# A recurrence in a two-layer decoder step: earlier masked queries in the first chunk, and 17 filler steps moved to the last two chunks

## The chip, the cores and the metric

The kernel runs on one core of a Trainium2 chip. The metric is the device time of one execution in microseconds (us), and less is better. Five engines work side by side: TensorE (PE in the profile) multiplies matrices, VectorE (DVE) and ScalarE (ACT) do element-wise work, GpSimd (POOL) does some of it and issues DMAs, SyncE (SP) issues DMAs.

## What is computed

One inference step of a decoder with two layers. The first mixes the sequence with a matrix-state recurrence, the second with attention; a feed-forward part follows each. Only the first mixer matters here. The reference, cut to it:

```
p = xn @ w_in                       # q, k, v, output gate og, two small gates
C = w_c * C + sum_s w_g[s] * k[s] v[s]^T           # state, per chunk of the sequence
num = w_inter * (q @ C) + (q k^T * exp(decay)) @ v
h = num / max(|den|, exp(-m))
out = (rmsnorm(h) * sigmoid(og)) @ w_out
```

There are 8 heads with 64-wide keys and 128-wide values. The sequence is a lead-in of 16 rows and a prompt of 1024; beside it go 8 decode requests of 8 rows, each with a state of its own.

## The kernel before, in words

**The stage.** `recurrence` works through nine chunks. Chunk 0 has 80 rows (the 64 rows of the decode requests and the lead-in), chunks 1 to 8 have 128 rows each. For the rest of a chunk the steps are, in the order in which they are written:

- `chunk_scores`: q k^T into PSUM (`sps`, L1349), times the decays (`eb`, DVE, L1351); the keys transposed (`kps`, L1355) and weighted (`kw`, DVE, L1357); the queries scaled (`wb`, DVE, L1359). The scores of chunk i+1 are made before the output of chunk i.
- `chunk_state`: keys times values into PSUM (`cp`, L1388), added to the state `C` (DVE, L1392); the new state is multiplied by the chunk's decay on POOL (L1395) for the chunk after it.
- `chunk_out`: scores times values (`nps`, L1450) plus queries times state (L1454), two pairs of heads at a time; the denominators (`den`, DVE, L1412) and values (`vA`, ACT, L1420) are copied out, the exponentials of a later chunk follow (L1335), then the squares for the norm (L1469, `jk`).

Every third chunk `norm_heads` normalizes three chunks (L1528 to L1539, DVE).

**The first chunk** also serves the 8 decode requests, each with its own state. `first_queries` writes the scaled queries `wb` to a DRAM tile `qwD` (L1367, POOL), loads them back as `q2` in another layout with four DMAs (L1371, POOL) and clears two masked-query tiles (L1373, POOL; all of them are called `qq` in the profile). In `chunk_out` the DVE copies a head's part of `q2` into such a masked tile (L1433), and four matmuls per head multiply it with the requests' states (`nps<-C,qq`, L1438).

**The fills.** The products of the output gate, `p[og]`, are not made in a phase of their own. `gates_out` is a generator: 8 weight blocks (`whi`, `wlo`: a high and a low part, made from `wraw` at L256 to L260) by 3 column groups (336, 384 and 384 columns) by 8 contraction steps, 192 steps in all. A call `f(n)` in the recurrence puts n steps into PE's program at that place. A step is three matmuls (L193, L194, L195, into `mmA`). Behind the eighth step of a group, ACT takes the sigmoid from PSUM (`stg`, L955) and POOL writes it to DRAM (`ogD`, L956).

**The gates.** With the last chunks, `gate_head` (L1555) transposes one head's normalized values of three chunks into PSUM (`ghps`, three matmuls), DVE multiplies them by the stored sigmoid (L1556, into `ogqk` or `ogeb`, loaded at L971), and ACT and DVE split the result into two parts `xh`, `xl` (L271, L272), which the output projection reads. Ten gates stand in chunks 7 and 8. Gates and fills take their PSUM tiles from the same two banks: while a group of fills is unfinished it holds one of them, and all gates go through the other.

**What follows.** `mlp` loads the output weights (`wo` and `slot` from `woD`, L512, SP), eight pairs of 512 KB loads in a fixed order, and multiplies them (`pops`, L193 to L195). The tiles `wo` lie where the recurrence had its tiles: the first pair in the place of the last fill block's `wlo`, the third in the place of the `stg` tiles. So SP's first load waits for the last fill, and its third pair for the writes of the last sigmoids to `ogD`.

**The order.** PE, DVE, ACT and POOL run the recurrence in the order in which the code is written (`manual_schedule`); each engine works its own list in order and waits on semaphores. A place of an `f(n)` is thus a place in PE's list, and of its sigmoid and `ogD` write in ACT's and POOL's.

Of the kernel before, what the change touches and what calls it, by code (L numbers as in the profile page):

```python
# [12 lines left out]
ALU = mybir.AluOpType  # L13
# [4 lines left out]
P = 128  # L18
D = 1024
KT = D // P  # L20
# [8 lines left out]
NT = len(TT)  # L29
# [849 lines left out]
@_add(Net)  # L879
def phase_a(self, vt):  # L880
    nc, I, O = self.nc, self.I, self.O
    w_in = I["w_in_a"][0]
    qkD = self.dram.tile([8, P, T], F32, name="qkD")
    ogD = self.dram.tile([8, P, T], F32, name="ogD")
# [266 lines left out]
@_add(Net)  # L1151
def recurrence(self, kp, rec, v, qkD, fill, gate):


    nc, I, O = self.nc, self.I, self.O
    eD, wD, cap, cap0, wcP, wcS, bm = rec
    tm, den, ssq = self.fin

    self.fills = 0

    def f(n):
        for _ in range(n):
            next(fill, None)
            self.fills += 1

    C = self.C
    E = mybir.EngineType
    with ExitStack() as cr, self.pool("recAp", bufs=2, space=PSUM) as pp:
        order = ExitStack()
        order.enter_context(self.tc.manual_schedule(engines={E.PE, E.DVE, E.Activation, E.Pool}))  # L1170
        args = (pp, kp, C, v, qkD, eD, wD, tm)

        r0 = cr.enter_context(self.pool("rec0"))
        sets = {1: r0}
        load = lambda i: self.chunk_load(i, sets[i % 3], *args)
        with self.pool("sampA") as sp:
            R = self.chunk_load(0, r0, *args)
            N = dict(eb=r0.tile([P, HA, P], F32, name="eb1", tag="eb", bufs=2))
            self.first_load(R, sp)
            f(4)  # L1180
            self.chunk_decay(0, R, tm, cap0)
            R["exp"]()
            f(6)
            self.chunk_scores(0, R, r0, *args, f)
            self.first_queries(R, sp)
            f(2)
            self.first_sums(R, pp)
            self.first_keys(0, R, bm)
            f(3)
            self.chunk_state(0, R, *args, wcP, f)  # L1190
            N = self.chunk_load(1, r0, *args, **N)
            self.chunk_out(0, R, r0, *args, den, ssq, f, sp)

            ahead = r0.tile([P, HA, P], F32, name="eb2", tag="eb", bufs=2)
            nc.gpsimd.dma_start(ahead, eD[:, TT[2][0] : TT[2][1]].partition_broadcast(P))
            self.first_states(R, sp, pp, v, wcS, bm, f, self.decay_steps(1, N, tm, cap), N)
        with self.pool("rec2") as sets[2], self.pool("rec1", bufs=2) as rp, self.pool("rec3") as sets[0]:
            R, N = N, self.chunk_load(2, sets[2], *args, eb=ahead, loaded=True)
            self.chunk_decay(2, N, tm, cap)
            N["exp"]()  # L1200
            f(10)
            self.chunk_scores(1, R, rp, *args, f)
            g, norm = f, iter(())
            places = []
            gate = gate(places)
            for i in range(1, NT):
                N2 = load(i + 2) if i + 2 < NT else None
                if i + 1 < NT:
                    f(12 if i == 1 else 3)
                    self.chunk_scores(i + 1, N, rp, *args, f)  # L1210
                next(norm, None)
                g(2)
                self.chunk_state(i, R, *args, wcP, g)
                if i == NT - 1:
                    state = self.last_state(C[i % 2], pp, rp)
                    next(state)
                if N2:
                    self.chunk_decay(i + 2, N2, tm, cap)
                next(norm, None)
                self.chunk_out(i, R, rp, *args, den, ssq, g, exp=N2 and N2["exp"],  # L1220
                               then=(lambda: next(state, None)) if i == NT - 1 else None)
                for _ in norm:
                    pass
                norm = self.norm_heads(i // 3, v, rp) if i % 3 == 2 else iter(())
                if i in (6, 7):

                    for x in ("qk", "eb"):
                        y = sets[i % 3].tile([P, 1024], F32, name=f"og{x}{i}", tag=x,
                                             bufs=2 if x == "eb" and i == 7 else None)
                        places += [y[:, z : z + GL] for z in (0, 512)]  # L1230
                    gate(-1)
                if i == 6:
                    while self.fills < 3 * KT * KT - KT:
                        f(1)

                    def g(n):
                        if i == NT - 1:
                            f(2)
                        gate(0) or gate(1)
                R, N = N, N2  # L1240
            f(1000)
            order.close()
            for _ in norm:
                pass
# [93 lines left out]
@_add(Net)  # L1338
def chunk_scores(self, i, R, rp, pp, kp, C, v, qkD, eD, wD, tm, f):

    nc = self.nc
    L = TT[i][1] - TT[i][0]
    qk, eb, qw = R["qk"], R["eb"], R["qw"]

    sps = [pp.tile([P, 4, P], F32, name=f"sps{i}{g}", tag="sps") for g in range(2)]
    for j in range(4):
        for g in range(2):
            r = slice(g * 64, g * 64 + 64)
            nc.tensor.matmul(sps[g][:L, j, :L], qk[r, 4 + j, :L], qk[r, j, :L], start=True, stop=True)  # L1349
    for g in range(2):  # L1350
        nc.vector.tensor_tensor(out=eb[:L, g::2, :L], in0=sps[g][:L, :, :L], in1=eb[:L, g::2, :L], op=ALU.mult)  # L1351
    f(2 if i else 6)
    kps = pp.tile([P, 4, P], F32, name=f"kps{i}", tag="sps")
    for j in range(4):
        nc.tensor.transpose(kps[:L, j, :], qk[:, 4 + j, :L], self.ident)  # L1355
    kw = R["kw"]
    nc.vector.tensor_tensor(out=kw[:L], in0=kps[:L].rearrange("p j (a k) -> p (j a) k", a=2),  # L1357
                            in1=tm[:L, i, 64:72].unsqueeze(2).broadcast_to([L, HA, DK]), op=ALU.mult)
    nc.vector.tensor_tensor(out=qw[:, :, :L], in0=qk[:, :4, :L], in1=qw[:, :, :L], op=ALU.mult)  # L1359


@_add(Net)
def first_queries(self, R, sp):

    nc = self.nc
    qd = self.dram.tile([P, 4, NS], F32, name="qwD")
    nc.gpsimd.dma_start(qd, R["qw"][:, :, :NS])  # L1367
    q2 = R["q2"]
    for a in range(2):
        for z in range(2):  # L1370
            nc.gpsimd.dma_start(q2[a * 64 : a * 64 + 64, :, z, :], qd[z * 64 : z * 64 + 64])  # L1371
    for qm in R["qms"]:
        nc.gpsimd.memset(qm, 0.0)  # L1373


@_add(Net)
def chunk_state(self, i, R, pp, kp, C, v, qkD, eD, wD, tm, wcP, f):

    nc = self.nc
    Cn, Cw = C[i % 2], C[2]  # L1380
    s = slice(NS, T0) if i == 0 else slice(0, P)
    for z in range(2):
        js = slice(2 * z, 2 * z + 2)
        ps = pp.tile([P, 2, DV + 1], F32, name=f"cp{i}{z}", tag="cps")
        for x in range(2):
            for a in range(2):
                h = 2 * (2 * z + x) + a
                nc.tensor.matmul(ps[a * 64 : a * 64 + 64, x, :], R["kw"][s, h, :], v(i)[s, h, :], start=True, stop=True)  # L1388
        if i == 0:
            nc.scalar.copy(Cn[:, js, :], ps)  # L1390
        else:
            nc.vector.tensor_tensor(out=Cn[:, js, :], in0=Cw[:, js, :], in1=ps, op=ALU.add)  # L1392
    if i + 1 < NT:

        nc.gpsimd.tensor_tensor(out=Cw, in0=Cn, in1=wcP[:, :, i].unsqueeze(2).broadcast_to([P, 4, DV + 1]),  # L1395
                                op=ALU.mult)


@_add(Net)
def chunk_out(self, i, R, rp, pp, kp, C, v, qkD, eD, wD, tm, den, ssq, f, sp=None, exp=None, then=None):  # L1400
# [8 lines left out]
    def done(ps, g, hs):  # L1409

        hx = slice(hs[0], hs[0] + 3, 2)
        nc.vector.tensor_copy(den[:L, i, hx], ps[:L, :, DV])  # L1412
        if i == 0:
            y = R["y"][g]
            nc.scalar.copy(y[:L], ps[:L, :, :DV])
            nps.append((y, hx))
            for x, h in enumerate(hs):
                nc.scalar.activation(R["jk"][:L], y[:L, x], AF.Square, accum_out=ssq[:L, 0, h : h + 1])
        else:
            nc.scalar.copy(v(i)[:L, hx, :DV], ps[:L, :, :DV])  # L1420

    new = lambda g: pp.tile([P, 2, DV + 1], F32, name=f"nps{i}{g}", tag="nps")
    if i == 0:
        for g, hs in enumerate(((0, 2), (4, 6), (1, 3), (5, 7))):
            f(4)
            ps = new(g)
            for x, h in enumerate(hs):
                o = ps[:L, x, :]
# [8 lines left out]
                for j in range(4):  # L1437
                    nc.tensor.matmul(o, qm[:, j * T0 : (j + 1) * T0], R["C0"][:, j, h, :], start=False, stop=(j == 3))  # L1438
            done(ps, g, hs)
    else:  # L1440

        for z in range(2):
            f(2 if z == 0 else 3)
            if z:
                f(3)
            ps = [new(2 * z + a) for a in range(2)]
# [1593 lines left out]
```

## Time and profile before

| | us |
|---|---|
| time, median of 3 runs | 2832.24 (2831.84 to 2833.01) |
| profiled execution, its own time | 2829.72 |
| its span | 2828.0 |
| PE busy in the span | 2761.9 (98%) |
| the recurrence with its fills and gates, `sps` of chunk 0 to the first `pops` | 244.3 to 428.3 of the span |
| PE idle between 235 and 455 by the waits it names | 7.9 |

Times in a row are us from the start of the span. A row of the timeline shows start, duration, engine, line, operation, output, inputs and shape; a bracket at its end is the idle time of the engine ahead of it and what ended it. Neighbours of one kind are shown as one row with their count. `PEclk` is the granted TensorE clock, 1.00 being full speed.

### The profile page before, as it was taken

The page shows a single profiled execution, that of the slowest core. Times are in us where ns is not written, and L with a number is a line of the kernel's source. Part 1 is how long each engine was busy: PE and PEld are TensorE (multiplying, and loading weights), DVE is VectorE, ACT ScalarE, POOL GpSimd, SP SyncE. Part 2 cuts the span into 40 slices and gives each one's busy share as a digit, 9 for nine tenths or more (in the row PEclk, how much of TensorE's full clock was granted, in tenths as well). Part 3 has the DMA queues.
Part 4 walks back from the last instruction along what each step waited for, and adds up shares of the span by engine and source line. Part 5 has one row for each costly group of instructions (what it writes and reads, how often), then busy time and mean ns, then how long its engine had stood idle before and what let it go on. Part 6 is the DMA issues. An engine that isn't in the chain of part 4 may idle for free. (4 is left out here: it accounts for less than half of the span.)

```text
span 2828.0 us, 60538 instructions
## 1 busy us (share of the span) xinstructions
PE 2761.9 (98%) x23543; PEld 2650.3 (94%) x23543; DVE 1800.4 (64%) x4025; ACT 1177.3 (42%) x2299; POOL 836.0 (30%) x1313
## 2 busy tenths in 40 slices
PE   8999999999999999999999999999999999999998
PEld 8989889999999999999999888677999999999998
DVE  4632566888887765563455444777388888766556
ACT  5422453432322334443444445777343223323345
POOL 3122233132232332124453202544313223323111
PEclk9999999999999999999999999999999999999999
DMA  6666547245554375545444676442524555527556
GB/s 196 171 196 162 144 125 255 90 143 165 176 167 148 112 243 174 195 145 171 139 172 132 237 279 226 154 143 86 157 83 128 175 176 164 161 90 239 178 191 215
DMA packets 439001, 474.03 MB, mean 168 GB/s; under 512 B 41422, under 2 KB 365258, under 8 KB 437690
## 3 DMA queue, kind: packets, MB, share of 16 engines
q1 hardware_dynamic: 387522, 320.78, 36.8%
q0 software_dynamic: 43808, 143.17, 15.3%
q10 hardware_dynamic: 7384, 6.22, 0.7%
q8 instruction: 185, 3.03, 0.5%
q14 instruction: 102, 0.84, 0.1%
HBM read 322.84 MB, written 147.21 MB: 166 GB/s over the span
## 5 line engine op out<-in xcount | busy, mean ns | idle before, releaser
L1611 PE MATMUL m<-xh,slot 128*128 128x276 f32 x2752 | 541.3, 290 | 1.8 <-ACT fs L1640 1.8
L1611 PEld LDWEIGHTS m<-xh,slot 128*128 128x128 f32 x2752 | 440.4, 188 | 3.6 <-ACT fs L1640 2.2
L1611 PE MATMUL m<-xl,slot 128*128 128x276 f32 x1376 | 397.4, 289 | 0.0
L1611 PEld LDWEIGHTS m<-xl,slot 128*128 128x128 f32 x1376 | 259.1, 188 | 0.0
L193 PE MATMUL tmps<-slot,xh 128*128 128x256 f32 (+2 forms) x864 | 243.1, 281 | 0.0
L195 PE MATMUL tmps<-slot,xl 128*128 128x256 f32 (+2 forms) x864 | 240.6, 278 | 0.0
L194 PE MATMUL tmps<-slot,xh 128*128 128x256 f32 (+2 forms) x864 | 240.5, 278 | 0.0
L272 DVE TENSOR_TENSOR slot<-slot,slot 128x1024 fp32r<-128x1024 f32 x124 | 162.9, 1314 | 60.7 <-ACT slot L271 59.2
L271 ACT CAST slot<-slot 128x1024 fp32r<-128x1024 f32 x124 | 129.6, 1046 | 141.2 <-PE m L1611 111.7
L194 PEld LDWEIGHTS tmps<-slot,xh 128*128 128x128 f32 (+1 forms) x864 | 159.2, 184 | 0.1
L195 PEld LDWEIGHTS tmps<-slot,xl 128*128 128x128 f32 (+1 forms) x864 | 158.6, 184 | 0.0
L193 PEld LDWEIGHTS tmps<-slot,xh 128*128 128x128 f32 (+1 forms) x864 | 158.4, 183 | 0.2
L193 PE MATMUL mmA<-xh,whi 128*128 128x384 f32 (+1 forms) x384 | 135.1, 352 | 0.0
L194 PE MATMUL mmA<-xl,whi 128*128 128x384 f32 (+1 forms) x384 | 127.9, 333 | 0.0
L195 PE MATMUL mmA<-xh,wlo 128*128 128x384 f32 (+1 forms) x384 | 127.7, 333 | 0.0
L272 DVE TENSOR_TENSOR slot<-vA,slot 128x1024 fp32r<-128x1024 f32 (+1 forms) x59 | 82.2, 1396 | 32.6 <-ACT slot L271 31.5
L272 DVE TENSOR_TENSOR slot<-Ht,slot 128x1024 fp32r<-128x1024 f32 (+1 forms) x59 | 81.4, 1382 | 32.3 <-ACT slot L271 31.1
L271 ACT CAST slot<-Ht 128x1024 fp32r<-128x1024 f32 (+1 forms) x59 | 61.0, 1037 | 96.8 <-PE m L1611 92.9
L271 ACT CAST slot<-vA 128x1024 fp32r<-128x1024 f32 (+1 forms) x59 | 60.8, 1035 | 95.5 <-PE m L1611 90.5
L1715 DVE TENSOR_TENSOR ws<-ws 128x128 f32<-128x128 f32 x264 | 93.8, 355 | 8.9
L2862 ACT ACTIVATE s<-s,nb 128x272 f32<-128x272 f32 (+7 forms) x126 | 98.9, 786 | 0.0
L2897 ACT COPY th<-tp 128x768 f32<-128x768 f32 (+1 forms) x80 | 73.6, 920 | 53.7 <-PE tp L2889 30.5
(805 smaller groups left out, 8668.8 us busy)
## 6 DMA issues: line engine op xcount, KB each, us to landing
ws<-in_w_down SPq DMA_DIRECT2D x176, 128.0 KB, 2.8
sD<-ws SPq DMA_DIRECT2D x176, 128.0 KB, 2.3
slot<-sD SPq DMA_DIRECT2D x40, 512.0 KB, 4.2
slot<-in_w_gate_up SPq DMA_DIRECT2D x36, 512.0 KB, 3.9
kp<-in_cache_k SPq DMA_DIRECT2D x32, 512.0 KB, 6.7
vp<-in_cache_v SPq DMA_DIRECT2D x32, 512.0 KB, 5.1
vA<-in_w_gate_up SPq DMA_DIRECT2D x26, 512.0 KB, 4.4
Ht<-in_w_gate_up SPq DMA_DIRECT2D x26, 512.0 KB, 3.9
```

Source lines behind the costliest of these rows:

```text
L193: mm(ps, sh, mh, start=first, stop=False)
L194: mm(ps, sh, ml, start=False, stop=False)
L195: mm(ps, sl, mh, start=False, stop=last)
L271: self.nc.scalar.copy(hi, src)
L272: self.nc.vector.tensor_tensor(out=lo, in0=src, in1=hi.bitcast(F32), op=ALU.subtract)
L1611: nc.tensor.matmul(u.ps[h, b], w[p][:, k], x[q][:, k], start=first and k == i == 0, stop=k == 3 and i == 2, skip_group_check=True)
L1715: tt(out=o, in0=a, in1=b, op=ALU.subtract)
L2862: nc.scalar.activation(ss[z, u], ss[z, u], AF.Exp, bias=nb[:, z : z + 1], accum_out=sm[:, u, z : z + 1])
L2897: nc.scalar.copy(th.rearrange("p x z (u h q) -> p h (x z u) q", h=2, q=64)[:, :, :n], pt[:, :, :n])
```

## The change

Six edits, all in the recurrence:

1. The call ahead of the next chunk's scores goes from 12 to 10 steps (chunk 1) and from 3 to 2 (the others); the one ahead of a chunk's first outputs from 2 to 1 (chunks 1 to 6); in chunk 0 each of four groups from 4 to 3.
2. The loop that ran all fills but the last eight at once in chunk 6 is gone, and a gate in chunks 7 and 8 has `f(2)` ahead of it (before: in chunk 8 only).
3. In chunk 0 the scaling of the queries (`wb`) stands ahead of the keys' transposes and weighting instead of behind them.
4. In `first_queries` the two clears stand between the write of `qwD` and its four loads, and the loads are in the order in which the heads need them.
5. In chunk 0 POOL's scaling of the state is issued behind the second group of outputs instead of ahead of the first.
6. An unused name in `phase_a`.

```
-                    f(12 if i == 1 else 3)
+                    f(10 if i == 1 else 2)
...
                 if i == 6:
-                    while self.fills < 3 * KT * KT - KT:
-                        f(1)
 
                     def g(n):
-                        if i == NT - 1:
-                            f(2)
+                        f(2)
                         gate(0) or gate(1)
...
+    scale = lambda: nc.vector.tensor_tensor(out=qw[:, :, :L], in0=qk[:, :4, :L], in1=qw[:, :, :L], op=ALU.mult)
+    if i == 0:
+        scale()
     f(2 if i else 6)
...
-    nc.vector.tensor_tensor(out=qw[:, :, :L], in0=qk[:, :4, :L], in1=qw[:, :, :L], op=ALU.mult)
+    if i:
+        scale()
...
-    for a in range(2):
-        for z in range(2):
-            nc.gpsimd.dma_start(q2[a * 64 : a * 64 + 64, :, z, :], qd[z * 64 : z * 64 + 64])
     for qm in R["qms"]:
         nc.gpsimd.memset(qm, 0.0)
+    for z in range(2):
+        for a in range(2):
+            nc.gpsimd.dma_start(q2[a * 64 : a * 64 + 64, :, z, :], qd[z * 64 : z * 64 + 64])
...
-        nc.gpsimd.tensor_tensor(out=Cw, in0=Cn, in1=wcP[:, :, i].unsqueeze(2).broadcast_to([P, 4, DV + 1]),
-                                op=ALU.mult)
+        decay = lambda: nc.gpsimd.tensor_tensor(out=Cw, in0=Cn, in1=wcP[:, :, i].unsqueeze(2).broadcast_to(
+            [P, 4, DV + 1]), op=ALU.mult)
+        if i:
+            decay()
+        else:
+            R["decay"] = decay
...
-            f(4)
+            f(3)
...
+            if g == 1:
+                R["decay"]()
...
-            f(2 if z == 0 else 3)
+            f(1 if z == 0 else 3)
```

POOL in chunk 0, from the write of `qwD` on; first before, then with the change:

```order
L1367 DMA qwD<-wb_3080 512x1x64
L1371 DMA qq<-qwD 64x4x64 x4
L1373 MEMSET qq 128x400 x2
L1395 TENSOR_TENSOR C_107<-C_105,wcP 128x516
L1279 DMA qk_3246<-qkD 128x8x128
```

```order
L1369 DMA qwD<-wb_3080 512x1x64
L1372 MEMSET qq 128x400 x2
L1375 DMA qq<-qwD 64x4x64 x4
L1277 DMA qk_3245<-qkD 128x8x128
L1276 DMA eb_3086<-eD 128x8x128
L1281 DMA wb_3246<-wD 64x4x128 x2
L957 DMA ogD<-stg_3261 128x384
L1396 TENSOR_TENSOR C_107<-C_105,wcP 128x516
```

The clears moved ahead of the loads, and the scaling of the state behind them, three prefetches and an `ogD` write.

PE from the fifth gate to the sixth, between chunk 7's outputs and chunk 8's state; before, where the three `mmA` matmuls are the last fill step of all:

```order
L1555 MATMUL ghps_4818<-ident,vA 128x80
L1555 MATMUL ghps_4818<-ident,vA 128x128 x2
L193 MATMUL mmA_4666<-xh,whi_4353 128x384
L194 MATMUL mmA_4666<-xl,whi_4353 128x384
L195 MATMUL mmA_4666<-xh,wlo_4354 128x384
L1555 MATMUL ghps_4852<-ident,vA 128x80
L1555 MATMUL ghps_4852<-ident,vA 128x128 x2
```

With the change, where the first three finish a group (`mmA_4716`) and the next three begin the last one (`mmA_4824`):

```order
L1562 MATMUL ghps_4790<-ident,vA 128x80
L1562 MATMUL ghps_4790<-ident,vA 128x128 x2
L193 MATMUL mmA_4716<-xh,whi_4446 128x384
L194 MATMUL mmA_4716<-xl,whi_4446 128x384
L195 MATMUL mmA_4716<-xh,wlo_4447 128x384
L193 MATMUL mmA_4824<-xh,whi_4446 128x384
L194 MATMUL mmA_4824<-xl,whi_4446 128x384
L195 MATMUL mmA_4824<-xh,wlo_4447 128x384
L1562 MATMUL ghps_4828<-ident,vA 128x80
L1562 MATMUL ghps_4828<-ident,vA 128x128 x2
```

Two steps stand there now, and the group that they finish has its sigmoid (`stg_4821`) on ACT at this place, behind chunk 7's last cast and squares:

```order
L271 CAST xh<-ogqk_4647 128x336
L1476 ACTIVATE jk_4797,ssqA<-vA 128x128
L1476 ACTIVATE jk_4801,ssqA<-vA 128x128
L1476 ACTIVATE jk_4805,ssqA<-vA 128x128
L1476 ACTIVATE jk_4809,ssqA<-vA 128x128
L956 ACTIVATE stg_4821<-mmA_4716 128x384
L271 CAST xh<-ogqk_4647 128x336
L271 CAST xh<-ogeb_4648 128x336
```

PE at the end of the recurrence, from the last outputs of chunk 8 to the output projection (`pops`); before:

```order
L1454 MATMUL nps_4910<-C_106,wb_4546 128x129
L1454 MATMUL nps_4911<-C_106,wb_4546 128x129
L1555 MATMUL ghps_4924<-ident,vA 128x128 x3
L1258 MATMUL nnpP<-ident,nnP 4x128
L193 MATMUL pops_5037<-xh,wo_293_5007 128x276
L194 MATMUL pops_5037<-xl,wo_293_5007 128x276
L195 MATMUL pops_5037<-xh,wo_293_5007 128x276
```

With the change:

```order
L1461 MATMUL nps_4904<-C_106,wb_4492 128x129
L1461 MATMUL nps_4905<-C_106,wb_4492 128x129
L193 MATMUL mmA_4824<-xh,whi_4446 128x384
L194 MATMUL mmA_4824<-xl,whi_4446 128x384
L195 MATMUL mmA_4824<-xh,wlo_4447 128x384
L1562 MATMUL ghps_4924<-ident,vA 128x128 x3
L1256 MATMUL nnpP<-ident,nnP 4x128
L193 MATMUL pops_5037<-xh,wo_293_5007 128x276
```

The last fill step of all stands here now, one gate ahead of the projection. Of the 192 steps, 191 stood ahead of the first gate before; 175 do now (173 of them ahead of chunk 8's `kps`).

More of the change, by code (lines that the diff above doesn't have):

```diff
@@ L881, in phase_a @@
     nc, I, O = self.nc, self.I, self.O
+    E = mybir.EngineType
     w_in = I["w_in_a"][0]
```

## The prediction, made before the changed kernel ran

> **What bounds the kernel now.** I read the page first.
>
> ```profile
> span 2828.0 us, 60538 instructions
> PE 2761.9 (98%) x23543; PEld 2650.3 (94%) x23543; DVE 1800.4 (64%) x4025; ACT 1177.3 (42%) x2299; POOL 836.0 (30%) x1313
> ```
>
> PE is busy for 98% of the span, and the change removes no matmul and adds none. It can only change PE's idle time and the time PE runs at a lower clock. All six edits lie between the first chunk and the output projection, so I read PE's waits there, from 235 to 455 us (columns: waiting line and what it waited for; us in total, times, longest).
>
> ```profile
> PE nps L1438 <- POOL C L1395: 2.3, 1, 2.3
> PE ghps L1555 <- DVE ogeb L1556: 2.1, 2, 1.2
> PE ghps L1555 <- DVE ogqk L1556: 2.0, 3, 1.1
> PE nps L1450 <- ACT vA L1420: 1.5, 3, 1.0
> ```
>
> That is 7.9 us in four groups: the first chunk's masked queries (2.3), the ten gates (4.1) and the copies of outputs (1.5, of which 1.0 in chunk 8). So the tail of gates holds 5.1 us, the first chunk 2.3, the chunks between 0.5. The clock comes next, by stretches of 3.41 us (first number: the length, then PE's busy time; PEclk is the granted clock).
>
> ```profile
> 254.27:257.68 3.41, 1.56 (x11) 1.27 (x9) 0.99 (x1) 0.49 (x1) 3.41 (x6) 1.00 0.28 79
> 257.68:261.09 3.41, 2.93 (x13) 2.96 (x14) 1.12 (x4) 0.00 (x0) 3.41 (x6) 0.50 0.48 131
> 418.11:421.52 3.41, 2.26 (x27) 1.90 (x23) 1.75 (x10) 2.95 (x8) 0.49 (x2) 1.00 0.89 258
> 421.52:424.93 3.41, 1.51 (x12) 0.91 (x11) 2.61 (x9) 1.21 (x4) 2.31 (x4) 1.00 1.03 419
> 424.93:428.34 3.41, 3.41 (x21) 2.88 (x19) 1.82 (x5) 1.29 (x4) 0.00 (x0) 0.50 1.02 389
> ```
>
> Where PE was busy for 1.56 and 1.51 us of a stretch, the next one ran at half clock; where it was busy for 2.26, the next did not. A half-clock stretch with PE busy throughout costs half of 3.41, **1.7 us**; the one behind the first stall costs half of its busy 2.93, 1.5. The bill of before in this stage is 2.3 + 1.5 + 0.5 + 5.1 + 1.7 = **11.1 us**. I now write the same bill for the changed kernel.
>
> **The first chunk (edits 3, 4, 5, and f(4) to f(3)).**
>
> ```profile
> 247.29 0.88 DVE L1351 TENSOR_TENSOR eb<-sps,eb 80x320 f32<-80x320 f32 x2
> 249.55 0.48 DVE L1359 TENSOR_TENSOR wb<-qk,wb 128x320 f32<-128x320 f32 x1
> 249.33 0.54 POOL L956 DMA_DIRECT2D ogD<-stg  x1 [3.31 <-ACT stg L955]
> 250.84 0.74 POOL L1367 DMA_DIRECT2D qwD<-wb  x1 [0.97 <-DVE wb L1359]
> 253.51 2.48 POOL L1371 DMA_DIRECT2D qq<-qwD  x4 [1.92 <-DMA qwD<-wb]
> 255.97 0.82 POOL L1373 MEMSET qq<- 128x400 f32 x2
> 256.75 1.06 POOL L1395 TENSOR_TENSOR C<-C,wcP 128x516 f32<-128x516 f32 x1
> 256.69 2.21 DVE L1433 COPY qq<-qq 64x32 f32<-64x32 f32 x4 [5.56 <-DMA qq<-qwD]
> 253.47 0.34 PE L193 MATMUL mmA<-xh,whi 128*128 128x384 f32 x1
> 254.00 0.34 PE L193 MATMUL mmA<-xh,whi 128*128 128x384 f32 x1
> 258.16 1.98 PE L1438 MATMUL nps<-C,qq 128*80 128x129 f32 x8 [2.33 <-POOL C L1395]
> 261.16 1.04 PE L1438 MATMUL nps<-C,qq 128*80 128x129 f32 x8
> ```
>
> (The two `mmA` rows are the starts of two fill steps in a row: a step of 384 columns takes 0.52 us, and so one of 336 some 0.46.) The first masked product starts at 258.16, after 2.33 us of waiting, and takes 1.98 where the next takes 1.04: the half clock. The row names POOL's state scaling, but the chain behind it is longer: scaled queries (DVE), write to DRAM, landing, four loads, landing, copies into the masked tile. With edit 3 the scaled queries are there at about 248.6 (behind 247.29 + 0.88, and 0.48 of their own, instead of behind `kps` and `kw` at 249.55), and POOL then waits for nothing between its `ogD` write (249.33 + 0.54) and `qwD`: the whole 0.97 of its row goes. The landing of `qwD` and the loads move by as much. The clears (0.82) fall into the 1.92 us in which POOL waits for that landing, so they cost nothing there; were the landing earlier, they would cost 0.82. The loads go out one each 0.62 us (2.48 for 4), and the order lets the first head go on two of them: 256.69 less 0.97 gives the first data at 255.7, the two copies end near 256.2, and the scaling of the state no longer stands on POOL ahead of them. PE, with one fill step (0.46) less in this group, arrives at 258.16 - 2.33 - 0.46 = 255.4. The wait is **0.8 to 1.0**, I take 0.9, and too short for a half clock by the rows above. The gain is 2.3 + 1.5 - 0.9 = 2.9 us. The moved scaling of the state costs nothing: nothing in chunk 0 reads it, and the other half of chunk 0's outputs and the requests' states lie between it and chunk 1; without that cover it would cost its 1.06.
>
> **The middle chunks (one step less ahead of the scores, one less ahead of the outputs).** Two steps of 0.52 us, 1.04 per chunk, leave PE's list, while the element-wise chain stays.
>
> ```profile
> 372.58 0.72 PE L1454 MATMUL nps<-C,wb 64*128 64x129 f32 x8
> 376.77 1.29 DVE L1351 TENSOR_TENSOR eb<-sps,eb 128x512 f32<-128x512 f32 x2 [3.22 <-ACT eb L1335]
> 377.77 0.60 PE L1355 MATMUL kps<-ident,qk 128*128 128x128 f32 x4
> 377.98 1.22 DVE L260 TENSOR_TENSOR wlo<-wraw,whi 128x1024 fp32r<-128x1024 f32 x1
> 401.11 1.16 PE L1450 MATMUL nps<-vA,eb 128*128 128x129 f32 x8 [0.27 <-ACT vA L1420]
> ```
>
> From the end of a chunk's outputs (372.58 + 0.72 = 373.30) the exponentials take until 376.77, and `kps` overwrites a bank that L1351's first half (0.65) has to read: it can go at 377.4, 4.1 us behind the outputs. PE reached it at 4.47, and with a step less reaches it at 3.95. That is 0.15 to 0.25 us a chunk; for six chunks **1.2 us** (0 if the exponentials come sooner as well, 2 if also the state's matmuls wait). In the chunks with a norm (3 and 6) the outputs already waited for the copies (0.27 at 401.11, and as much in chunk 3: the two make 0.5 of the 1.5 us in the list of waits), so no cover is left: chunk 3 waits its 0.25 and most of the two steps, **1.1**; in chunk 6 the split of the last weight block (L260, 1.22 us on DVE), which stood earlier, now falls in as well, **1.8** (1.3 without it).
>
> **Chunks 7 and 8 (edit 2).** Here 18 steps, 9.4 us of PE work, come behind `kps` of chunk 8, two ahead of nearly every gate.
>
> ```profile
> 407.84 0.46 PE L1555 MATMUL ghps<-ident,vA 80*128 80x80 f32 x3
> 408.22 1.10 PE L1388 MATMUL cp<-vA,kw 128*64 128x129 f32 x16
> 415.73 0.51 PE L1555 MATMUL ghps<-ident,vA 80*128 80x80 f32 x3
> 428.31 0.38 PE L193 MATMUL pops<-xh,wo 128*128 128x276 f32 x1
> 409.84 0.47 ACT L271 CAST xh<-ogqk 128x336 fp32r<-128x336 f32 x1 [1.33 <-DVE ogqk L1556]
> 418.81 0.19 ACT L1469 ACTIVATION_READ_ACCUMULATOR jk<-vA 128x1 f32 x1
> 419.01 1.28 ACT L955 ACT_TABLE_LOAD   x1
> 420.30 0.49 ACT L955 ACTIVATE stg<-mmA 128x384 f32<-128x384 f32 x1
> ```
>
> The old waits of up to 1.2 us for a previous gate's DVE step are covered by two steps (1.04) but for some 0.15 at each of four gates, **0.6** in all (0 to 1). But two gates now need the bank of a group that has just ended, so they wait for a sigmoid. The second gate: ACT casts the first gate's head at 409.84, then loads its table (1.28) and runs the sigmoid (0.49), until 412.1; PE arrives 3.5 us behind 407.84 (two steps 1.04, gate 0.4, state 1.1, one step of each width 0.98) at 411.3: **1.0** with the hand-over. The sixth gate: its sigmoid stands behind chunk 7's squares, which end at 419.0, 3.3 us behind the fifth gate's start (415.73), and takes 0.49: 3.8. PE is there after the gate and two steps, some 1.7 us: **2.1**. A stretch around that wait may have PE busy for less than 1.6; I give a half clock there 0.7, so **1.1**.
>
> **The weights of the projection.**
>
> ```profile
> SPq L512 <- PE mmA L195: 37.5, 1, 37.5
> SPq L512 <- DMA ogD<-stg: 7.2, 1, 7.2
> DMA to landing us min/median/max: 9.4/9.4/9.4
> slot<-in_w_gate_up SPq DMA_DIRECT2D x36, 512.0 KB, 3.9
> ```
>
> SP's load of the first `wo` pair waited 37.5 us for PE's last fill step, and then had from 416.8 to 428.3 before PE needed it: 11.5 us, in which PE did the sixth to the tenth gate and chunk 8. Now the last step stands one gate (0.5 us) ahead of `pops`, so PE waits for the load. A 512 KB load takes 3.9 us elsewhere, and a second at 419 GB/s (the stretch at 421.52) 1.25 more: 5.2. The upper end is the 9.4 us of these very loads among others. The row of 3.9 has the same queue and size, and SP has nothing ahead of this pair, so I stay near the lower end: 5.3, less the gate 0.5, **4.8** (4.6 to 8.9). Such a gap halves the clock: **1.7**. The third pair waits for the last sigmoid's write to `ogD` (7.2 us of waiting in before), which now comes later too: **0.7** (0 to 3).
>
> **The sum.** After: 0.9 + 1.2 + 1.1 + 1.8 + 0.6 + 1.0 + 2.1 + 1.1 + 4.8 + 1.7 + 0.7 = 17.0 us, against 11.1: **+5.9 us**. From the profiled execution, 2829.7 (span 2828.0 and 1.7 around it), that is 2835.6; it lies 2.5 below the median of the runs, 2832.2, so for the median I forecast **2838.1**.
>
> The Trainium skill, "TensorE: Matmul & The Clock Gate", Part 1, has the clock halved after an idle window of about 3.4 us. The trace disagrees: a wait of 2.33 us sufficed. By the rule only the wait for the weights goes cold, the sum is 1.1 lower, 2837.0, just on the near side of the bound below.
>
> **The rivals.**
> - *The tail is filled, and the weights come in time* (not slower). If the first `wo` load doesn't hang on the last fill step, the 4.8 + 1.7 + 0.7 go, and if ACT runs the sigmoids early, 2.1 + 1.1 as well: 17.0 - 10.4 = 6.6, so -4.5, 2828; with the sigmoids waited for, -1.3, 2831. It decides at a landing within 0.5 us of the last step. For it: the idle gaps of the tail are real, 5.1 us. Against it: the 37.5 us row.
> - *The middle chunks keep their cover.* Where the exponentials move up with PE, the 1.2 + 1.1 + 1.8 stay at 0.5: +2.3, 2834.5. For it: `kps` had 0.4 us to spare. Against it: 0.4 is less than a step, and at 401.11 there was nothing to spare.
> - *The weights are late and stay late.* The load shares the queues (DMA share 1.03 at 421.52) and takes 9.4: 8.9 - 4.8 = 4.1 more, and with the third pair at 2 it is +11.3, 2843.5.
> - *The queries don't come sooner.* If the landings set the start and not the issue, the first chunk keeps 2.3 + 1.5: +2.9 on the forecast, 2841. The two landings in a row speak for it; the removed 0.97 against.
>
> **How the numbers follow.** The forecast 0.48 (2835 to 2841, half of it above the bound), the tail filled 0.14, the middle covered 0.14, the weights late 0.16, the queries late 0.08. The bound that a measurement of this kernel tells from no change is 0.2%, 5.7 us: above 2837.9 is slower, below 2826.6 faster. Faster takes the far part of the first rival, 0.06; slower is half of the forecast, the two late cases and a little from the rest, 0.52; the same 0.42. The range leaves out the far part of the filled tail and the worst of the late weights: 2830 to 2844.
>
> **What would show it.** In the changed profile: `nps<-C,qq` with a first wait of about 0.9 and no stretch at 0.50 behind it; `kps` waiting for L1351 in chunks 3 to 8; `ghps` waiting for ACT's `stg` twice, 1.0 and 2.1; `pops` waiting about 5 us for `wo`, and SP's `wo` issue directly behind the last `mmA`. If `pops` doesn't wait, the forecast is wrong, and by most of its size.

## The result, and the profile after

The changed kernel takes 2838.14 us in the median of 20 runs, the kernel before, in 20 runs beside it, 2831.02. The ratio is 1.0032, 95% interval 1.0026 to 1.0038: slower by 7 to 11 us (the plain medians differ by 7.1). One of the changed kernel's runs, at a granted clock of 0.85 throughout, is left out of the ratio. The profiled execution took 2840.86 us. Runs of one kernel spread over some 10 us, so single steps are read inside the traces and not from the totals.

The page of the changed kernel, and PE's waits from 235 to 465 us:

```profile
span 2839.1 us, 60536 instructions
PE 2766.7 (97%) x23543; PEld 2653.6 (93%) x23543; DVE 1799.5 (63%) x4025; ACT 1177.6 (41%) x2299; POOL 835.6 (29%) x1313
```

```profile
PE pops L193 <- DMA wo<-woD: 4.0, 1, 4.0
PE ghps L1562 <- ACT stg L956: 2.6, 2, 1.8
PE nps L1457 <- ACT vA L1425: 2.6, 2, 1.6
PE pops L195 <- DMA wo<-woD: 1.6, 1, 1.6
PE nps L1443 <- issue: 1.6, 1, 1.6
PE kps L1356 <- DVE eb L1349: 0.5, 2, 0.2
```

The same number of matmuls, but another list of waits. The old waits of gates for DVE are gone. In their place stand `pops` waiting for its weights (5.6) and two gates waiting for a sigmoid (2.6); two outputs wait longer for copies than before (2.6 in all), and the first chunk still waits 1.6.

Where the time went is best seen by stages cut at the same instructions: chunk 0 (first `sps` to that of chunk 1), chunks 1 to 8 up to chunk 8's `kps`, the gates up to the first `pops`, and the first two blocks of `pops`. Length, then PE busy; PEclk and DMA share stand near the end. Before:

```profile
244.34:308.34 64.00, 61.67 (x391) 54.18 (x390) 28.04 (x86) 19.51 (x40) 16.98 (x28) 0.97 0.45 119
308.34:407.40 99.06, 98.55 (x781) 89.59 (x781) 58.35 (x138) 55.20 (x154) 35.57 (x49) 1.00 0.46 133
407.40:428.31 20.91, 15.71 (x135) 12.58 (x134) 13.86 (x42) 10.67 (x35) 7.00 (x11) 0.92 0.59 204
428.31:434.76 6.45, 6.45 (x53) 6.45 (x52) 5.12 (x20) 3.80 (x12) 2.18 (x4) 1.00 1.03 398
```

With the change:

```profile
243.43:303.48 60.05, 58.44 (x378) 50.96 (x377) 29.28 (x86) 19.31 (x40) 17.09 (x28) 1.00 0.47 128
303.48:398.92 95.44, 92.37 (x739) 82.08 (x738) 58.69 (x138) 53.90 (x149) 34.39 (x47) 1.00 0.48 134
398.92:430.79 31.87, 25.15 (x188) 21.85 (x188) 17.95 (x58) 15.72 (x51) 9.92 (x17) 0.92 0.39 115
430.79:442.11 11.32, 9.70 (x52) 9.38 (x52) 4.47 (x7) 0.80 (x3) 0.37 (x1) 0.63 0.96 339
```

The four stages add up to 190.42 us before and 198.68 after: **+8.26 us**, within the 7 to 11 of the ratio. Steps were moved out of the first two (4 and 14, so 18 in all; 19 now stand behind chunk 8's `kps`, where one stood). The first is shorter by 3.95 us, about 2 of them for its four steps and the rest for the first chunk's edits; the second is shorter by 3.6 only, though 14 steps of some 0.5 us left it. The third took the steps in, and its idle time should have shrunk; it grew from 5.2 to 6.7. The fourth is the same 48 matmuls and a few transposes, and takes 4.9 us more, at a granted clock of 0.63.

The rows of the tail in the changed kernel, PE's idle time in brackets:

```profile
403.82 0.48 PE L1562 MATMUL ghps<-ident,vA 80*128 80x80 f32 x3 [0.80 <-ACT stg L956]
415.05 0.52 PE L1562 MATMUL ghps<-ident,vA 80*128 80x80 f32 x3 [1.79 <-ACT stg L956]
426.20 0.49 PE L1562 MATMUL ghps<-ident,vA 128*128 128x128 f32 x3
430.79 0.60 PE L193 MATMUL pops<-xh,wo 128*128 128x276 f32 x1 [4.00 <-DMA wo<-woD]
433.23 0.60 PE L195 MATMUL pops<-xh,wo 128*128 128x276 f32 x1 [1.61 <-DMA wo<-woD]
```

and SP's loads of the weights:

```profile
426.44 9.82 SPq L512 DMA_DIRECT2D wo<-woD  x6
```

What SP waited for ahead of them (it was 37.5 us in the kernel before):

```profile
SPq L512 <- PE mmA L195: 41.5, 1, 41.5
```

The last fill step ends at 426.4, SP issues the first load at 426.44, and PE reaches `pops` at 426.8. The load's high part is there at 430.8, the low part at 433.2.

### The profile page after: what moved, and what is told of

Same layout as the page of the kernel before. It is cut to its first block, busy times and chain, and to the rows that moved or that the text cites. A ratio compares the mean times of both kernels' runs of the same rounds, so it can differ in the third digit from the quotient of the medians.

```text
span 2839.1 us, 60536 instructions
## 1 busy us (share of the span) xinstructions
PE 2766.7 (97%) x23543; PEld 2653.6 (93%) x23543; DVE 1799.5 (63%) x4025; ACT 1177.6 (41%) x2299; POOL 835.6 (29%) x1313
## 5 line engine op out<-in xcount | busy, mean ns | idle before, releaser
L194 PE MATMUL tmps<-slot,xh 128*128 128x256 f32 (+2 forms) x864 | 240.9, 279 | 0.0
L194 PEld LDWEIGHTS tmps<-slot,xh 128*128 128x128 f32 (+1 forms) x864 | 159.3, 184 | 0.1
L194 PE MATMUL mmA<-xl,whi 128*128 128x384 f32 (+1 forms) x384 | 127.5, 332 | 0.0
```

What stands on the lines that cost most here:

```text
L194: mm(ps, sh, ml, start=False, stop=False)
```

## Experiments

Each kernel was run in five rounds against the kernel before on the same chip. Because parts with the same instructions differ by microseconds from one execution to the next (the first `sps` came between 242.3 and 246.9 us in these profiles), the table gives, beside the ratio, the stage from the first `sps` to the fifth block of `pops`, read from each kernel's own trace. That is one execution of each. In every row it lies inside what the ratio's interval gives, but up to 2.4 us from its middle, so differences of a microsecond or two between rows are not certain.

| kernel | ratio to before (95%) | stage, us | against before |
|---|---|---|---|
| before | 1 | 197.2 | |
| the change | 1.0032 (1.0026 to 1.0038) | 205.4 | +8.2 |
| first chunk's edits only | 1.0010 (1.0001 to 1.0018) | 201.0 | +3.8 |
| moved fills only | 1.0031 (1.0018 to 1.0043) | 208.4 | +11.2 |
| change, first pair elsewhere | 1.0027 (1.0018 to 1.0036) | 204.1 | +6.9 |
| before, last step late | 1.0021 (1.0011 to 1.0031) | 203.5 | +6.3 |
| change, middle calls of before | 1.0016 (1.0006 to 1.0026) | 201.8 | +4.6 |
| first chunk's edits, end as before | 0.9998 (0.9989 to 1.0008) | 197.8 | +0.6 |
| change, tiles turned | 1.0043 (1.0029 to 1.0056) | 209.5 | +12.2 |
| change, steps gone by the 7th gate | 1.0012 (1.0003 to 1.0020) | 201.4 | +4.2 |
| first chunk's edits, step at the 5th gate | 1.0011 (1.0001 to 1.0020) | 199.5 | +2.3 |
| change, steps gone by the 5th gate | 1.0021 (1.0009 to 1.0032) | 201.4 | +4.2 |
| before, step at the 5th gate | 1.0010 (1.0000 to 1.0019) | 201.6 | +4.4 |
| first chunk's edits, 5th gate, last write on ACT | 0.9995 (0.9986 to 1.0004) | 195.9 | -1.3 |

**My theory** was that the last fill step's place sets when the weights come, and that this is the largest part of the loss. **The rival** was that the loss comes from lost cover in the middle chunks and from the sigmoid waits.

### One step moved, and nothing else

The kernel before, with only the last step put where the change has it:

```
                         if i == NT - 1:
-                            f(2)
+                            self.gates = getattr(self, "gates", 0) + 1
+                            f(2 if self.gates == 5 else 0)
                         gate(0) or gate(1)
```

> The kernel before, with one fill step moved: the last one stands ahead of the last gate, where the change has it, instead of ahead of the sixth gate. Nothing else differs. My theory: pops waits 4 to 6 us for wo and runs at half clock behind it; 5 to 9 us slower than before. Rival, that the loss of the change comes from the cover lost in the middle chunks and the waits for sigmoids: within 1.5 us of before.

It is slower as expected: a ratio of 1.0021, and 6.3 us in the stage. PE's waits in it:

```profile
PE pops L193 <- DMA wo<-woD: 4.9, 1, 4.9
PE pops L195 <- DMA wo<-woD: 1.1, 1, 1.1
```

One step of 0.52 us, moved four gates later, makes 6.3 us, where the whole change makes 8.2 and its moved fills without the first chunk's edits 11.2 (next section). The rival is left with the rest, up to 4.9 us, in which the lost cover and the sigmoid waits were not told apart by a run of their own; two of the kernels below differ in the moved calls of the middle chunks and the gates' steps alone and are 1.9 us apart (201.4 and 199.5).

### The halves of the change

First chunk's edits only (the middle calls, the loop and the gates as in the kernel before):

```
-                    f(10 if i == 1 else 2)
+                    f(12 if i == 1 else 3)
...
+                    while self.fills < 3 * KT * KT - KT:
+                        f(1)
...
-                        f(2)
+                        if i == NT - 1:
+                            f(2)
```

> Only the first chunk's edits (queries scaled sooner, clears ahead of the loads, state scaling behind, f(3) per group); the calls in the middle chunks, the loop in chunk 6 and the gates as before. My theory: the stage of chunk 0 gains about 2 us (in the changed kernel it is 3.95 us shorter, of which four fewer steps make 2.1), no stretch at half clock behind the first masked product, and three steps are left for chunk 8's gates, where they fill idle time: 1 to 4 us faster than before. Rival, that the queries' head start is given back at the next wait: within 1 us of before.

Moved fills only:

> Only the moved fill steps (calls of 10, 2, 1 and 3 steps, no loop, two steps ahead of every gate); the first chunk's queries, clears, loads and scaling as before. My theory: all of the loss and none of the gain, 8 to 12 us slower than before, with pops waiting 4 to 7 us for wo. Rival, that the first chunk's edits themselves cost time later: less slow than the whole change, under 7 us.

The second came out as expected: all of the loss, 2.8 us of the first chunk's wait back, `pops` waiting 4.9 us, +11.2 in the stage. Against the whole change that is 3.0 us more, so the first chunk's edits are worth some 3 us there. The totals can't tell the two apart (1.0031 and 1.0032, with intervals of 0.0006 and more either way).

The first was a miss. It should have been faster and was slower, by 2.8 us in time and 3.8 in the stage. Its waits:

```profile
PE pops L193 <- DMA wo<-woD: 3.1, 1, 3.1
PE pops L195 <- DMA wo<-woD: 1.7, 2, 1.2
```

None of this is for the first pair of weights. The second pair's low part takes 0.5, at 426.65; the other 4.3 are for the third pair, at 433.17 and 434.94, and SP's list says what held it:

```profile
SPq L512 <- PE mmA L195: 35.5, 1, 35.5
SPq L512 <- DMA ogD<-stg: 9.0, 1, 9.0
```

In the kernel before, 186 steps were done when it came to the loop in chunk 6, which so had nothing to run. With four steps fewer in chunk 0 it ran two, up to its bound of 184, and three steps were left for the gates instead of one. The last step came one gate later, and the write of its sigmoid with it. The third pair's tile lies over that `stg` tile, and SP issues in order: it waited 9.0 us for the write.

### The end as before, and no gain

```
-                    while self.fills < 3 * KT * KT - KT:
+                    while self.fills < 3 * KT * KT - KT + 2:
```

> The first chunk's edits alone again, but the loop in chunk 6 runs two more steps, so that one step is left as in the kernel before and stands at the same gate (the sixth). In the run with three steps left, the third pair of weights waited for the last sigmoid's write and came 4.3 us late. My theory: without that the chunk's gain stays, no wait of pops for wo, 1 to 3.5 us faster than before. Rival, that any gain ahead of the weights is given back there: pops waits 1 us or more, within 1 us of before.

```profile
PE pops L195 <- DMA wo<-woD: 1.5, 1, 1.5
PE pops L193 <- DMA wo<-woD: 0.9, 1, 0.9
```

The diff is against the run with the first chunk's edits only. The rival had it. From the first `sps`, the first `pops` came 3.8 us sooner (180.1 us behind it, 184.0 before), and the fifth block 0.6 us later: the third pair was 2.4 us late again, and a stretch at a granted clock of 0.54 followed (437.4 to 440.8). PE came 3.8 us sooner and found the pair 2.4 us late. If it landed in the kernel before at the same distance from the first `sps`, it had some 1.4 us to spare there, and a gain beyond that is lost; this is an estimate, as no row shows that landing. By it the kernel before was bound here by the weights nearly as much as by PE.

### Trying to free the weights

First by the tiles. Changed kernel, with the first pair in the tile behind:

```
-                ws = [ws[x] for x in (3, 2, 1, 0)] + held if heads else held + ws
+                ws = [ws[x] for x in (2, 3, 1, 0)] + held if heads else held + ws
```

> The changed kernel, with the first two of the four wo tiles exchanged, so that the first pair of weights lies over the last raw weight block, which is free since chunk 6, and the second over the last fill block's low part. My theory: SP's first pair no longer waits for the last fill step, pops begins right behind the last gate, and only the second pair can be late, by 0 to 2 us: 5 to 8 us faster than the changed kernel, within 3 us of before. Rival, that the queues are full and the loads late anyway: pops still waits 3 us or more, under 2 us gained.

It tells nothing on the question: the tile lies over the high part of the same weight block, and SP waited for the step just the same ("PE mmA L194", 41.4 us, the second matmul of the last step instead of the third). The other end of the list, `(0, 3, 2, 1)`:

> The changed kernel with the order of the four wo tiles turned (the fourth first), so that the first pair of weights needs neither the last fill step nor the last sigmoid; the second pair waits for the last step and the fourth for the last sigmoid's write. (The earlier exchange put the first pair over the high part of the same last block, so it lifted nothing.) My theory: pops starts right behind the last gate, the second pair is 1 to 2.5 us late and the fourth up to 4, with part of the half clock left: 1 to 5 us faster than the changed kernel. Rival, that the queues are the limit and not the two waits: no gain.

Neither theory: there was no gain, as the rival said, but not for its reason, and the stage is 4.0 us longer than the change's. SP's row and PE's:

```profile
SPq L512 <- DMA ogD<-stg: 94.8, 1, 94.8
```

```profile
PE pops L193 <- DMA wo<-woD: 8.8, 1, 8.8
PE pops L195 <- DMA wo<-woD: 1.0, 1, 1.0
```

This tile needs the `ogD` writes too, so now the first pair waits for the last sigmoid's write, and `pops` waits 9.8 us instead of 5.6. It shows the second chain by itself: step, sigmoid, write, load.

Then by the steps. The changed kernel with `f(3 if i == 7 else 2)` ahead of the gates, so that the last step stands at the seventh:

> The changed kernel with three steps instead of two ahead of each gate of chunk 7, so that the last step stands ahead of the seventh gate instead of the tenth; all else as in the changed kernel. My theory: pops waits under 1.5 us for the first pair instead of 5.6, but the third pair, which waits for the last sigmoid's write, is 1 to 4 us late: 2 to 5 us faster than the changed kernel, 2 to 6 slower than before. Rival, that the loss lies in the waits ahead of the projection: under 1 us gained.

```profile
PE pops L193 <- DMA wo<-woD: 2.7, 1, 2.7
PE pops L195 <- DMA wo<-woD: 2.2, 2, 1.7
```

4.0 us of the stage are gained by three gates' distance, as expected. `pops` doesn't wait for the first pair at all; the second pair's low part is 1.7 us late, and the third pair 3.2. With the middle calls of the kernel before, the last step stands at the third gate:

> The changed kernel with the calls of before in the middle chunks (12, 3 and 2 steps), so that only 5 steps are left behind kps of chunk 8 and the last one stands ahead of the third gate, three gates earlier than in the kernel before. My theory, that the last step and the write of its sigmoid set when the weights come: no wait of pops for wo, the waits for a sigmoid gone (no group but the last ends among the gates), chunks 3 and 6 at 0.3 us each again, the first chunk's gain kept: 2 to 6 us faster than before. Rival, that chunk 0's gain is lost to something else (the run with the first chunk alone was not faster): within 1.5 us of before or slower.

```profile
PE ghps L1562 <- DVE ogqk L1563: 4.5, 1, 4.5
```

No wait for weights, but a new one, which I had not thought of: a gate waits for its own stored sigmoid. POOL issued the gates' loads at 413.2 and after, SP 2 MB of weights from 411.8 on, and the small loads came behind the large ones: a median of 6.9 to 7.2 us from issue to landing, by kind of load, where the first such loads of the kernel before (issued at 412.7 to 416.6) took 2.6 to 2.9. With four steps ahead of each gate of chunk 7, `f(4 if i == 7 else 2)`, and with the two kernels whose one step goes to the fifth gate, the same:

```
                         self.gates = getattr(self, "gates", 0) + 1
                         if self.gates > 4:
                             f(2)
```

> The changed kernel with four steps ahead of each gate of chunk 7 instead of two, so that the last step stands at the fifth gate and its sigmoid ahead of the squares; the middle calls are those of the change. My theory: the late weights go (pops waits under 1.5 us), what is left is the cover lost in the middle chunks (3.1 us idle there against 0.5): 5 to 9 us faster than the changed kernel, within 2 us of before. Rival, throughput of the queues: pops waits 2 us or more, under 4 us gained.

> The first chunk's edits alone, one step left for the gates, and that step at the fifth gate instead of the sixth: on ACT the last sigmoid then stands ahead of chunk 7's squares, with its table loaded already, and SP's first pair goes one gate sooner. In the run with this step at the sixth gate, pops came 3.9 us sooner and lost 4.4 of it to the third pair, which waits for the last sigmoid's write. My theory, that this write is the limit: the write lands 2 us or more sooner, the waits of pops for wo fall from 2.4 to under 1 us, 1.5 to 4 us faster than before. Rival, that the queues' throughput is the limit: pops waits 2 us or more again, within 1.5 us of before.

> The kernel before with its one late step at the fifth gate instead of the sixth, nothing else changed; a control for the two others. My theory: pops waited for no weights in the kernel before, so there is nothing to gain but the 0.3 us wait of the sixth gate: within 1 us of before. Rival, that this place alone makes a kernel faster or slower (weights ahead of the gates' own loads): more than 1.5 us either way.

The waits of gates for DVE in the three, in that order:

```profile
PE ghps L1562 <- DVE ogeb L1563: 4.0, 1, 4.0
```

```profile
PE ghps L1566 <- DVE ogeb L1567: 5.3, 2, 4.1
```

```profile
PE ghps L1556 <- DVE ogeb L1557: 6.0, 2, 4.8
```

`pops` waited for no weights in any of them, as I expected, but all three lost 4.0 to 4.8 us at one gate, and the time of none came out as its theory said: the changed kernel with its steps gone by the fifth gate gained 4.0 us of the stage and not 5 to 9, and the other two were slower than before. The control's rival had it, that this place alone makes a kernel slower: the kernel before with its step one gate sooner is 4.4 us longer in the stage (by the ratio 0 to 5). POOL in the second of them shows why:

```profile
418.98 0.55 POOL L957 DMA_DIRECT2D ogD<-stg  x1 [3.79 <-ACT stg L956]
419.76 1.06 POOL L972 DMA_DIRECT2D ogeb<-ogD  x2 [0.23 <-issue]
```

The write of the last sigmoid stands on POOL ahead of the gates' last loads and waits for ACT, and the loads wait behind it. The last kernel takes this write off POOL:

```
-                            nc.gpsimd.dma_start(ogD[m, :, t0:t1], s[:, :n])
+                            (nc.scalar if (m, t) == (7, 2) else nc.gpsimd).dma_start(ogD[m, :, t0:t1], s[:, :n])
```

> The first chunk's edits, the last step at the fifth gate, and the last sigmoid's write to ogD issued by ACT instead of POOL. With that write on POOL the loads of the gates' stored sigmoids stood behind it, went out 3 to 4 us later, behind 2 MB of weights, and a gate waited 4.1 us for them. My theory, that POOL's order and not the throughput made that wait: the gate's wait falls under 1 us, pops waits under 1.5 us for wo, 1 to 4 us faster than before. Rival, that the weights take the queues whoever issues first: gate or pops still waits 3 us or more, within 1.5 us of before or slower.

```profile
411.80 0.54 POOL L972 DMA_DIRECT2D ogeb<-ogD  x1 [1.12 <-DVE xl L272]
413.32 0.54 POOL L972 DMA_DIRECT2D ogeb<-ogD  x1 [0.99 <-DVE den L1421]
```

```profile
PE ghps L1566 <- DVE ogeb L1567: 2.7, 2, 1.5
```

The loads go out as their buffers come free, the gate's wait falls from 4.1 to 1.5 (two waits share the 2.7), not below the 1 us of the theory, `pops` waits for nothing, and the stage is 1.3 us shorter than before: the only one of the twelve that is. In time it is 0.9995 (0.9986 to 1.0004), which is not told from no change. So POOL's order made most of that wait. The rest goes with the queues: the load issued at 411.80 landed after 2.5 us, the one issued at 413.32, together with SP's first weights, after 5.0; how much faster this end could be with less DMA traffic was not tried.

## Why the prediction was right

The forecast was 2838.1, and the way to it holds: it is slower because the last fill step holds the weights. That it meets the median of 2838.14 to a tenth is luck. The sum gave +5.9 us, where the medians differ by 7.1 and the stages by 8.3, and the kernel before, taken at 2832.2, came out 1.2 lower in 20 runs. Within the sum, too, errors cancel: the terms put too high come to 2.8 us, those put too low to 3.4. By its own terms, predicted and read from the changed kernel's trace:

| term | predicted, us | measured, us |
|---|---|---|
| first chunk's wait | 0.9 | 1.6 |
| `kps` behind the scores | 1.2 | 0.5 |
| chunk 3, chunk 6 | 1.1, 1.8 | 1.0, 1.6 |
| gates behind DVE | 0.6 | none |
| second gate, sixth gate behind a sigmoid | 1.0, 2.1 | 0.8, 1.8 |
| half clock behind the sixth gate | 1.1 | 1.4 |
| `pops` behind the first pair | 4.8 | 5.6 |
| half clock behind it | 1.7 | 3.3 |
| third pair | 0.7 | none |
| sum | 17.0 | 17.6 |

The third pair was in time there, it seems, because the first one was late: in the three kernels in which the first was in time and the last step stood at the seventh gate, or at the sixth with the first chunk's edits, the third was late (2.4 to 4.3 us), as the term feared. With the last step at the fifth gate or the third no pair was. The sum less the 11.1 of before gives 6.5 us, and the stage grew by 8.3. The other 1.8 us are no wait: in the four stages above PE's busy time grew from 182.4 to 185.7 for the same matmuls, and half clock explains only 1.5 of that (3.2 before, 4.7 after). What in it takes longer stays open.

**The first chunk.** `nps<-C,qq` starts without a half clock behind it, as forecast, but waits 1.6 and not 0.9:

```profile
247.18 0.48 DVE L1350 TENSOR_TENSOR wb<-qk,wb 128x320 f32<-128x320 f32 x1
249.54 0.74 POOL L1369 DMA_DIRECT2D qwD<-wb  x1 [0.58 <-issue]
252.53 2.48 POOL L1375 DMA_DIRECT2D qq<-qwD  x4 [1.44 <-DMA qwD<-wb]
255.37 0.97 DVE L1438 COPY qq<-qq 64x32 f32<-64x32 f32 x3 [0.33 <-DMA qq<-qwD]
256.02 1.08 PE L1443 MATMUL nps<-C,qq 128*80 128x129 f32 x8 [1.56 <-issue]
```

The queries are ready at 247.7, but POOL still stands idle 0.58 us ahead of `qwD`, where I had the whole 0.97 go; the row names no wait for it. From the issue of `qwD` to the loads it is 2.99 us, where it was 2.67, and the clears did fall into that time (1.44 left of 1.92). The gain is 2.3 + 1.5 - 1.6 = 2.2 us by this bill, where I had 2.9, and 3.0 by the run without the edits.

**The mis-sized step: the half clock behind the weights, 1.7 predicted and 3.3 measured.** The stretches there, in the changed kernel:

```profile
424.20:427.60 3.40, 2.60 (x23) 2.02 (x21) 2.51 (x9) 1.73 (x5) 0.12 (x1) 1.00 0.90 292
427.60:431.00 3.40, 0.21 (x1) 0.21 (x2) 2.22 (x12) 3.28 (x11) 2.45 (x5) 0.71 0.95 297
431.00:434.40 3.40, 1.79 (x7) 1.46 (x8) 3.13 (x5) 0.17 (x1) 0.16 (x1) 0.50 0.98 355
434.40:437.80 3.40, 3.40 (x17) 3.40 (x17) 0.85 (x1) 0.00 (x0) 0.00 (x0) 0.50 0.87 303
437.80:441.20 3.40, 3.40 (x23) 3.40 (x23) 0.44 (x1) 0.43 (x1) 0.00 (x0) 0.79 1.03 363
```

I had reckoned with one stretch. The pair came in two halves, so behind the 4.0 us came two matmuls and another 1.6 us of waiting, and the clock, down since about 429, stayed at half until about 439: the first two blocks of `pops` took 9.7 us of work instead of 6.45.

**The rule on the clock.** Around the sixth gate, two more stretches of the changed kernel:

```profile
410.60:414.00 3.40, 2.52 (x15) 1.85 (x13) 1.68 (x8) 2.14 (x9) 1.61 (x3) 1.00 0.65 193
414.00:417.40 3.40, 2.35 (x19) 1.85 (x19) 1.87 (x8) 1.35 (x6) 0.55 (x1) 0.70 0.21 76
417.40:420.80 3.40, 3.40 (x25) 3.23 (x25) 1.31 (x5) 0.47 (x1) 1.30 (x2) 0.80 0.31 59
```

A wait of 1.79 us was enough for the clock to fall; it cost 0.30 of 2.35 and 0.20 of 3.40, 1.4 us. The waits of 1.56 us in chunk 0 and 1.6 us in chunk 6 were not: PEclk is 1.00 over both of those stages. The Trainium skill ("TensorE: Matmul & The Clock Gate", Part 1) would have needed an idle window of about 3.4 us, so the trace disagrees once more. It also shows the limit of how I read the windows of before: stretches cut at other places have PE busy for 2.3 to 2.5 of 3.4 here, so a threshold of 1.6 holds for that cut only.

**The rivals.** "The weights come in time" was wrong at the row that spoke against it, SP's wait for the last step (41.5 us now). "The middle keeps its cover" was wrong by the 3.1 us that PE stood idle there, against 0.5. "The weights are late and stay late" had the load take 9.4 us; its high part was there 4.4 us behind the issue and its low part 6.8. "The queries don't come sooner" was wrong in the main: no half clock followed the first wait, but 1.6 us of it stayed.

## What to carry to other kernels

- Ask of a step that is moved not only what waits for its result but what waits for its buffers. Here the last reader of a weight tile, and the write of its last output, held the next phase's loads; 0.5 us of work four gates later cost 6 us.
- A place in a program can be narrow on both sides: one gate later the weights were late, one gate sooner the gates' own small loads came behind 2 MB of weights. When a gain ahead of such a place comes to nothing, look at what has to be there at its end.
- Where runs of a kernel spread over more than an edit is worth, compare stages between equal instructions in the traces, and use the totals for the verdict alone.

## What the runs showed of the hardware that was not expected

Two DVE operations on chunk 0's keys (`km<-kw,bm`) took 0.86 us together before and 2.02 with the change, where POOL's clears (0.91) run beside them:

```profile
250.19 0.91 POOL L1372 MEMSET qq<- 128x400 f32 x2
249.35 2.02 DVE L1483 TENSOR_SCALAR km<-kw,bm 64x512 f32<-64x512 f32 x2
```

It cost nothing, as DVE then idled until 254.86. All ten kernels with the clears moved show 2.01 or 2.02, the four without 0.86 or 0.87. That the clears caused it is argued from the overlap and was not tried; the issue of `qwD` (249.54) falls beside these operations too.
